# An unused tile that moves the squared activations by 640 bytes

## The chip, the cores and the metric

The kernel runs on one core of a Trainium2 chip. Its metric is device time, from the start of the program to its end, in microseconds (us). Three runs of the kernel before took 2282.85, 2284.05 and 2285.39 us; the median is 2284.05 us. Below, PE is the tensor engine (PEld its weight loads), DVE the vector engine, ACT the scalar engine, SP the engine whose queue issues the DMAs.

## The reference

Two layers of a decoder trunk on 256 tokens with 2048 features, in float32. Per layer:

```
mod = silu(c) @ w_ada + b_ada              # shift, scale, gate for the mixer and for the MLP
h   = rms_norm(x, g_pre_mix) * (1 + scale_a) + shift_a
y   = concat(mLSTM(h @ w_in), attention(h @ w_in)) @ w_out
x   = x + gate_a * rms_norm(y, g_post_mix)
h   = rms_norm(x, g_pre_mlp) * (1 + scale_m) + shift_m
y   = square(relu(h @ w_up)) @ w_down      # 2048 -> 8192 -> 2048
x   = x + gate_m * rms_norm(y, g_post_mlp)
```

The change is in the place of what `square(relu(h @ w_up))` is kept in. The two MLPs hold most of the arithmetic.

## The kernel before, in words

**Products in three parts.** Every large weight matrix streams from DRAM in loads of 1 MiB (128 partitions by 2048 columns, tile `raw`). A load is split in two slabs; of each slab, ACT makes a rounded copy `whi` (line 232) and DVE the rest `wlo = raw - whi` (line 236), both 128 by 1024 elements in the type float32r. Activations are kept in the same way, as a high and a low part. A product is the sum of three matmuls: high by high, low by high, high by low (lines 326 to 330, `products`; the matmul is line 329). Four tiles each of `whi` and `wlo` rotate, six of `raw`.

**Two forms of a unit.** A unit is one block of 512 weight columns, accumulated in two PSUM banks. In `body_xs` (line 332) the activations are stationary, 128 features by 128 tokens (512 bytes in each partition), and 512 columns of the slab move past them: this is the form of the output projection (`op`), of the down-projection (`dn`) and of a few units of the in-projection (`vm`, `om`). In `body_ws` (line 338) 128 columns of the slab are stationary and 256 tokens of the activations move: the form of the up-projection (`up`). Each matmul is preceded by the load of its own stationary operand.

**Order.** One list fixes the order of all loads, slabs and units. In the MLP the units alternate: for each of 8 stages `e`, one up unit (a block of 512 hidden features, 16 k-tiles), four down units (`dn`, 8 k-tiles each, one for each 512 output features), one more up unit. After an up unit, `evac_up` (line 1007) evacuates it: ACT takes the relu into the tile `r` and squares it into `sh`; DVE squares `r` in place and writes `sl = r - sh`. The down units read `sh` and `sl` as their stationary operands. In between, DVE also sums rows of `w_ada` (line 204), adds up the outputs of the down units (line 1064), and SP issues the loads.

**Where the tiles lie.** Pools are stacked in each partition's memory in the order in which they are opened. `raw`, `whi`, `wlo` and the normed activations `ht` (which also hold the concatenated heads, `cth` and `ctl`) lie one behind the other, each tile a whole number of 4096 bytes; all of them begin 1504 bytes into a page of 4096 bytes. Behind them come pools of other sizes, 32128 bytes together. Then the pools that live for one phase alone. For the MLP these are the two opened at lines 997 and 998:

```
sp = mlp.enter_context(tc.tile_pool(name="s" + L, bufs=3))   # sh, sl: six tiles of 4096 bytes
rp = mlp.enter_context(tc.tile_pool(name="r" + L, bufs=2))   # r: two tiles of 2048 bytes
```

Since 32128 is 640 less than eight pages, the six tiles of `sp` begin 864 bytes into a page, in both layers, and the two of `rp` at 864 and 2912. A stationary operand in `ht` begins 1504 bytes into a page plus a multiple of 512, one in `sp` 864 bytes plus a multiple of 512; the 512 columns of a slab begin at 1504 or 3552.

Of the kernel before, what the change touches and what calls it, by code (L numbers as in the profile page):

```python
# [7 lines left out]
F32 = mybir.dt.float32  # L8
# [6 lines left out]
PSUM = bass.MemoryType.PSUM  # L15
# [11 lines left out]

# column offsets in the packed small parameters
NL = 234
# [3 lines left out]

# shape-only constants: identity | banded distances | causal bias
K_ID, K_DIST, K_CAUS = 0, 128, 512
# [4 lines left out]
def hymba_kernel(ctx: ExitStack, tc: tile.TileContext, x_d, c_d, cols_d, cons_d, wada_d,  # L40
# [48 lines left out]

    # instructions behind which the splits and the sums of w_ada queue on their engine, lest they come  # L90
    # between the steps of a norm that the tensor engine waits for
    hold = {"hi": None, "lo": None, "ada": None}

    def rsqrt(ssq, n_over, n, name):
        """1 / sqrt(ssq / n_over + eps): an estimate from the exponent bits and three Newton steps."""
        v, y, t = [smp.tile([P, n], F32, tag=f"rs_{a}", name=f"{name}_{a}") for a in "vyt"]
        V.tensor_scalar(v, ssq, 1.0 / n_over, EPS, ALU.mult, ALU.add)
        V.tensor_scalar(y.bitcast(I32), v.bitcast(I32), -0.5, 1597463007.0, ALU.mult, ALU.add)
        V.tensor_scalar(v, v, -0.5, None, ALU.mult)
        for _ in range(3):  # L100
            if n == 1:
                V.tensor_scalar(t, y, y, v, ALU.mult, ALU.mult)
            else:
                V.tensor_tensor(t, y, y, ALU.mult)
                V.tensor_tensor(t, t, v, ALU.mult)
            last = V.scalar_tensor_tensor(y, t, 1.5, y, ALU.add, ALU.mult)
        hold["ada"] = last.ins
        return y

# [1 line left out]
    # ("w", blocks of (unit, first k-tile), source) of weights; ("a", layer, vector, pair of feature tiles) of w_ada  # L111
    SHA, SCA, GTA, SHM, SCM, GTM = range(6)
# [8 lines left out]
    def weave(ws, *segments):  # L121
        """ws, with the entries ads of each segment (ads, start, upto) spread evenly over that range of ws."""
        at = {}
        for ads, start, upto in segments:
            for k, a in enumerate(ads):
                at.setdefault(start + int(k * (upto - start) / len(ads)), []).append(a)
        for n, w in enumerate(ws):
            plan.append(w)
            plan.extend(at.pop(n, []))
        assert not at  # L130
# [32 lines left out]

    # each entry in two loads
    loads, subs, ada_fifo = [], [], []
# [13 lines left out]

# [1 line left out]
    LA, RING, AHEAD = 2, 4, 5  # L181
# [16 lines left out]
    def ada_op():  # L198
        """Sums over the input features for one tile of 128 output features."""
        k, l, v, j = ada_fifo.pop(0)  # L200
        load_to(k + AHEAD)
        w = raws[k]
        with behind("ada"):
            V.scalar_tensor_tensor(w, w, 1.0, cact, ALU.mult, ALU.mult, accum_out=modc[l][:, v, j:j + 1])  # L204
        n = modn[l, v] = modn.get((l, v), 0) + 1
        gate = v in (GTA, GTM)
        if n % (KT if gate else 2):
            return
        j0 = 0 if gate else n - 2
        m = modc[l][:, v, j0:n]  # L210
        V.tensor_tensor(m, m, lcol(l, O_BA + 16 * v + j0, n - j0), ALU.add)
        if v in (SCA, SCM):
            g = lcol(l, (O_GPM if v == SCA else O_GPL) + j0, n - j0)
            V.scalar_tensor_tensor(m, m, 1.0, g, ALU.add, ALU.mult)
        if gate:
            V.tensor_tensor(m, m, lcol(l, O_GQM if v == GTA else O_GQL, KT), ALU.mult)
# [31 lines left out]

# [1 line left out]
    class Task:  # L250
# [36 lines left out]
    class Unit:  # L287
        """Products with one block of 512 weight columns, accumulated in two PSUM banks."""

# [21 lines left out]
        def slabs_by_token(self, between):  # L311
            """Four slabs, all for the first token tile and then all for the second."""
            prefill(RING)
            four = [take() for _ in range(4)]
            for s in four:
                side()
                self.mm(s, toks=(0,))
            between()
            for s in four:
                self.mm(s, toks=(1,))  # L320
# [33 lines left out]

    # gate rows (times the post-norm gain) broadcast over the partitions
    gps = {}
# [14 lines left out]

# [1 line left out]
    class PreNorm:  # L373
        """Residual update (with yg), RMSNorm, modulation and transposition of x."""

# [33 lines left out]
        def group(self, g, tok):  # L409
            """Transposed activations of four k-tiles, in two parts."""  # L410
            tag, l = self.tag, self.l
# [17 lines left out]
        def turn_in(self, xnT, tok, g0=0):  # L429
            """Transposition of one token tile from k-tile 4 g0 on, before the modulation is known."""  # L430
            for g in range(g0, 4):
                ps = xalloc(f"pst{self.tag}_{g}_{tok}")
                for k in range(4):
                    T.transpose(ps[:, k * P:(k + 1) * P], self.xn[g, tok][:, k * P:(k + 1) * P], ident)
                o = xnT[g][:, :, TK[tok]]
                p4 = ps.rearrange("p (k t) -> p k t", k=4)
                if g % 2:
                    A.activation(o, p4, AF.Copy)
                else:
                    V.tensor_copy(o, p4)  # L440
                xdone()

        def modulate(self, e, xnT, hfp):
            """Two k-tiles of the activations."""
            tag, l, g = self.tag, self.l, e // 2
# [20 lines left out]
    def turn(last_mm, evac, nrm, make, staged=None):  # L466
        """Between two phases: the token tiles pass one after the other through the end of the last
        unit, the norms and the start of the first unit of the next phase. The first half of the
        k-tiles goes through all the units made, then the second half."""
        def mid():  # L470
# [35 lines left out]

# [1 line left out]
    crow = gpp.tile([P, D], F32, tag="gp", name="crow")[0:1, :]  # L508
# [15 lines left out]
    for l in range(DEPTH):  # L524
# [34 lines left out]

# [1 line left out]
        ha = {}  # L561
# [61 lines left out]
        def swa_out(g, po):  # L623
            """Normalisation of four heads and their sums of squares."""
            hs = slice(4 * g, 4 * g + 4)
# [59 lines left out]

# [1 line left out]
        def conv_silu(ps, u, out_scale):  # L687
# [24 lines left out]

# [1 line left out]
        wg = tp.tile([P, KT, 8], F32, tag="wg", bufs=1, name=f"wg{L}")  # L714
# [5 lines left out]
        def gates():  # L720
# [28 lines left out]
            xdone()  # L749
            # log sigmoid(f) = min(f, 0) - log1p(exp(-|f|)), log1p(t) = log(w) + (t - (w - 1)) / w with w = 1 + t  # L750
            V.scalar_tensor_tensor(t1, fg, -1.0, fg, ALU.mult, ALU.min)
# [14 lines left out]
            yield  # L766
            # u = i - b, g = running maximum of u (from the stabiliser before the chunk), m = b + g
            u_, m_, emm, g_, ub = both[0:4], lf, fg, t2, t1
# [8 lines left out]
            yield  # L777
            # columns: u (two chunks), u + B (first chunk), exp(-m) (two chunks)
            while live["x"] > 3:
# [8 lines left out]

# [1 line left out]
        va = {}  # L790
# [13 lines left out]
        def mlstm_weights(h):  # L804
            """exp(u_s - g_t) times q k, [source position, target position]."""
            pg = xalloc(f"pg{L}_{h}")
# [81 lines left out]

# [1 line left out]
        cg = {}  # L890
# [28 lines left out]

# [1 line left out]
        if l:  # L921
# [33 lines left out]

# [1 line left out]
        cT = lambda kt: (cg[kt // 4][0][:, kt % 4, :], cg[kt // 4][1][:, kt % 4, :])  # L957
# [35 lines left out]

# [1 line left out]
        hT2 = PreNorm("m" + L, l, SCM, SHM, yg, ssy)  # L995
        mlp = ExitStack()
        sp = mlp.enter_context(tc.tile_pool(name="s" + L, bufs=3))
        rp = mlp.enter_context(tc.tile_pool(name="r" + L, bufs=2))
# [22 lines left out]
        def evac_up_tokens(un, u):  # L1021
            """As evac_up, for products with tokens on the partitions."""
            ps = un.ps
# [180 lines left out]
```

## Time and profile before

| | |
|---|---|
| three runs, median | 2284.05 us (2282.85 to 2285.39) |
| profiled execution, span from first to last instruction (the page gives no other time for it) | 2283.6 us |
| mean granted clock of the tensor engine | 0.987 of full |
| PE, PEld, DVE, ACT busy | 96%, 85%, 74%, 48% of the span |
| chain that ended last, `up` and `dn` matmuls | 31.7% and 30.8% of the span |
| DMA | 590.08 MB, 258 GB/s mean |

The page gives the busy time of each engine. Matmuls are pipelined: the duration shown of one is its time from start to end, and the next has begun by then. How many fit in a stretch is read from the starts, or from the chain of waits, which lists stretches of one kind of instruction with their count. A "pitch" below is the time from one start to the next.

### The profile page before, as it was taken

The page shows a single profiled execution, that of the slowest core. Times are in us where ns is not written, and L with a number is a line of the kernel's source. Part 1 is how long each engine was busy: PE and PEld are TensorE (multiplying, and loading weights), DVE is VectorE, ACT ScalarE, POOL GpSimd, SP SyncE. Part 2 cuts the span into 40 slices and gives each one's busy share as a digit, 9 for nine tenths or more (in the row PEclk, how much of TensorE's full clock was granted, in tenths as well). Part 3 has the DMA queues.
Part 4 walks back from the last instruction along what each step waited for, and adds up shares of the span by engine and source line. Part 5 has one row for each costly group of instructions (what it writes and reads, how often), then busy time and mean ns, then how long its engine had stood idle before and what let it go on. Part 6 is the DMA issues. An engine that isn't in the chain of part 4 may idle for free.

```text
span 2283.6 us, 33092 instructions
## 1 busy us (share of the span) xinstructions
PE 2195.6 (96%) x13322; PEld 1935.3 (85%) x13322; DVE 1690.7 (74%) x2282; ACT 1090.9 (48%) x1533; POOL 1.4 (0%) x14
## 2 busy tenths in 40 slices
PE   6789999899999999999989999989999999999998
PEld 5679777698898998989869988878898998998986
DVE  7988899787878877877577797957556656555556
ACT  4346663645444444434464566556443444444433
POOL 0000000000000000000000000000000000000000
PEclk9999999999999999999999999999999999999999
DMA  9997679497888888888538766845656666555551
GB/s 370 385 360 273 221 300 365 171 356 307 315 299 336 308 309 312 316 305 300 185 128 336 294 223 215 294 165 197 234 213 230 229 223 248 203 185 186 184 187 70
DMA packets 82363, 590.08 MB, mean 258 GB/s; under 512 B 9185, under 2 KB 9633, under 8 KB 10785
## 3 DMA queue, kind: packets, MB, share of 16 engines
q1 hardware_dynamic: 82210, 587.98, 69.4%
q8 instruction: 104, 1.70, 0.3%
q14 instruction: 49, 0.40, 0.0%
HBM read 585.81 MB, written 2.13 MB: 257 GB/s over the span
## 4 chain that ended last, share of the span: by engine, by line
PE 77%; DVE 4%; ACT 1%; issue 1%; DVEq 0%; ACTq 0%
PE up L329 32%; PE dn L329 31%; PE op L329 4%; PE qa L329 2%; PE vm L329 2%; PE om L329 1%; PE km L329 1%; PE qm L329 1%; PE kva L329 1%; DVE x L388 1%; DVE wlo L236 1%; PE pss L592 0%; PE pss L591 0%; ACT jkm L84 0%; PE psgate L730 0%
## 5 line engine op out<-in xcount | busy, mean ns | idle before, releaser
L236 DVE TENSOR_TENSOR wlo<-raw,whi 128x1024 fp32r<-128x1024 f32 x720 | 876.6, 1222 | 472.2 <-ACT whi L232 470.9
L232 ACT ACTIVATE whi<-raw 128x1024 fp32r<-128x1024 f32 x720 | 758.5, 1058 | 915.3 <-PE dn L329 376.0
L329 PE MATMUL up<-hthm,whi 128*128 128x256 f32 x1920 | 543.7, 283 | 0.0
L329 PE MATMUL up<-hthm,wlo 128*128 128x256 f32 x1920 | 543.3, 283 | 0.0
L329 PE MATMUL up<-htlm,whi 128*128 128x256 f32 x1920 | 543.2, 283 | 0.0
L204 DVE SCALAR_TENSOR_TENSOR raw<-raw,cact 128x2048 f32<-128x2048 f32 x192 | 437.3, 2285 | 4.1 <-DMA raw<-in_wada_dram 4.0
L329 PE MATMUL dn<-whi,sh 128*128 128x512 f32 x1024 | 404.1, 395 | 0.0
L329 PE MATMUL dn<-wlo,sh 128*128 128x512 f32 x1024 | 404.0, 395 | 0.0
L329 PE MATMUL dn<-whi,sl 128*128 128x512 f32 x1024 | 404.0, 395 | 0.0
L329 PEld LDWEIGHTS up<-htlm,whi 128*128 128x128 f32 x1920 | 368.4, 192 | 0.9
L329 PEld LDWEIGHTS up<-hthm,whi 128*128 128x128 f32 x1920 | 368.4, 192 | 0.9
L329 PEld LDWEIGHTS up<-hthm,wlo 128*128 128x128 f32 x1920 | 368.4, 192 | 0.0
L329 PEld LDWEIGHTS dn<-wlo,sh 128*128 128x128 f32 x1024 | 192.9, 188 | 45.0
L329 PEld LDWEIGHTS dn<-whi,sh 128*128 128x128 f32 x1024 | 193.0, 188 | 44.7 <-ACT sh L1034 0.4
L329 PEld LDWEIGHTS dn<-whi,sl 128*128 128x128 f32 x1024 | 192.9, 188 | 44.4 <-DVE sl L1035 0.2
L329 PE MATMUL op<-wlo,cth 128*128 128x512 f32 x256 | 99.6, 395 | 2.8 <-DVE wlo L236 2.8
L329 PE MATMUL op<-whi,cth 128*128 128x512 f32 x256 | 99.2, 396 | 2.6 <-ACT whi L232 2.6
L329 PE MATMUL op<-whi,ctl 128*128 128x512 f32 x256 | 100.2, 393 | 0.0
L329 PE MATMUL vm<-whi,htha 128*128 128x512 f32 x128 | 57.0, 447 | 28.7 <-ACT whi L232 18.7
L1064 DVE TENSOR_TENSOR ys<-ys,dn 128x512 f32<-128x512 f32 x112 | 75.4, 685 | 5.2 <-PE dn L329 4.6
L329 PE MATMUL qa<-htha,whi 128*128 128x256 f32 x256 | 73.2, 286 | 0.0
L329 PE MATMUL qa<-htla,whi 128*128 128x256 f32 x256 | 72.4, 283 | 0.0
(275 smaller groups left out, 2545.1 us busy)
## 6 DMA issues: line engine op xcount, KB each, us to landing
raw<-in_wada_dram SPq DMA_DIRECT2D x192, 1024.0 KB, 6.4
raw<-in_wdn_dram SPq DMA_DIRECT2D x128, 1024.0 KB, 5.0
raw<-in_wup_dram SPq DMA_DIRECT2D x120, 1024.0 KB, 4.9
raw<-in_win_dram SPq DMA_DIRECT2D x56, 1024.0 KB, 5.0
raw<-in_wout_dram SPq DMA_DIRECT2D x32, 1024.0 KB, 6.8
raw<-in_wst_dram SPq DMA_DIRECT2D x16, 1024.0 KB, 6.6
raw<-in_wsu_dram SPq DMA_DIRECT2D x8, 1024.0 KB, 6.2
gp<-gdr SPq DMA_DIRECT2D x4, 1024.0 KB, 4.7
```

What stands on the lines that cost most here:

```text
L204: V.scalar_tensor_tensor(w, w, 1.0, cact, ALU.mult, ALU.mult, accum_out=modc[l][:, v, j:j + 1])
L232: A.activation(hi, raw, AF.Copy)
L236: V.tensor_tensor(lo, raw, hi.bitcast(F32), ALU.subtract)
L329: T.matmul(o, a, w, start=not self.started[b], stop=last and i == 2, skip_group_check=True)
L388: V.scalar_tensor_tensor(xc, self.yg[c][tok], r, xc, ALU.mult, ALU.add)
L1064: V.tensor_tensor(yt, yt, ps[tok], ALU.add)
```

## The change

Ahead of the pool of the squared activations, a pool is opened that holds one tile of 160 float32 (640 bytes) in each partition. No instruction reads or writes it. It is open as long as the MLP of its layer. The pools `sp` and `rp` lie 640 bytes further up: the six tiles of `sp` begin 1504 bytes into a page, the two of `rp` at 1504 and 3552. No other tile moves. The rest of the diff takes comments away.

```
         hT2 = PreNorm("m" + L, l, SCM, SHM, yg, ssy)
         mlp = ExitStack()
+
+        mlp.enter_context(tc.tile_pool(name="page" + L, bufs=1)).tile([P, 160], F32, name=f"page{L}")
         sp = mlp.enter_context(tc.tile_pool(name="s" + L, bufs=3))
         rp = mlp.enter_context(tc.tile_pool(name="r" + L, bufs=2))
```

On all five engines the same instructions stand in the same order as before, with the same waits; only the addresses of `sh`, `sl`, `r` and of the tiles that borrow their places in layer 0 (`xnT`, `hfs`) differ.

## Rows read from the trace of the kernel before

**Rows 1.** The page: busy time and share of each engine.
```profile
PE 2195.6 (96%) x13322; PEld 1935.3 (85%) x13322; DVE 1690.7 (74%) x2282; ACT 1090.9 (48%) x1533; POOL 1.4 (0%) x14
```

**Rows 2.** The chain that ended last, stretches: start us, length us, what, count.
```profile
533.12 0.44 PE up L1032 x4
533.55 44.87 PE dn L329 x192
601.46 44.62 PE dn L329 x192
...
1122.63 39.05 PE dn L329 x168
...
1465.47 58.96 PE op L329 x259
...
1660.62 46.07 PE up L329 x384
...
2160.21 44.62 PE dn L329 x192
2204.83 23.03 PE up L329 x192
2227.86 39.05 PE dn L329 x168
```

**Rows 3.** Who waited for whom: engine, line, releaser; us in total, times, longest.
```profile
ACT whi L232 <- PE dn L329: 376.0, 224, 1.7
ACT whi L232 <- PE up L329: 355.3, 200, 1.9
```

**Rows 4.** One down stage, PE: durations min/median/max in ns, first and last start.
```profile
L329 PE MATMUL dn<-whi,sh x64: 390/393/404, 1706.5 to 1750.4; 128*128 128x512 f32 x64
L329 PE MATMUL dn<-whi,sl x64: 390/393/404, 1706.8 to 1750.7; 128*128 128x512 f32 x64
L329 PE MATMUL dn<-wlo,sh x64: 390/393/404, 1707.0 to 1750.9; 128*128 128x512 f32 x64
```

**Rows 5.** The same view of the output projection of layer 1.
```profile
L329 PE MATMUL op<-whi,ctl x84: 389/389/393, 1467.1 to 1523.8; 128*128 128x512 f32 x84
L329 PE MATMUL op<-wlo,cth x84: 389/389/389, 1467.4 to 1523.3; 128*128 128x512 f32 x84
L329 PE MATMUL op<-whi,cth x83: 389/389/389, 1467.6 to 1523.6; 128*128 128x512 f32 x83
```

**Rows 6.** Timeline of weight loads in a down stage: start us, length us, what.
```profile
1625.13 0.19 PEld L329 LDWEIGHTS dn<-wlo,sh 128*128 128x128 f32 x1
1625.37 0.19 PEld L329 LDWEIGHTS dn<-whi,sh 128*128 128x128 f32 x1
1625.60 0.19 PEld L329 LDWEIGHTS dn<-whi,sl 128*128 128x128 f32 x1
...
1626.76 0.19 PEld L329 LDWEIGHTS dn<-whi,sh 128*128 128x128 f32 x1
1627.00 0.19 PEld L329 LDWEIGHTS dn<-whi,sl 128*128 128x128 f32 x1
```

**Rows 7.** Stretches: start:end, length, busy us (count) by engine, clock, DMA share, GB/s.
```profile
783.00:827.50 44.50, 44.50 (x193) 36.09 (x192) 37.85 (x43) 18.56 (x20) 0.00 (x0) 1.00 0.87 323
1467.00:1524.00 57.00, 57.00 (x253) 47.19 (x252) 34.66 (x35) 24.70 (x33) 0.00 (x0) 1.00 0.70 250
1706.70:1751.30 44.60, 44.60 (x194) 36.15 (x194) 30.87 (x31) 18.66 (x20) 0.00 (x0) 1.00 0.65 235
```

**Rows 8.** DVE lines: shapes, count | busy us, mean ns | idle before.
```profile
L1016 DVE TENSOR_TENSOR sl<-r,sh 128x512 fp32r<-128x512 f32 x60 | 41.3, 689 | 1.2
L427 DVE TENSOR_TENSOR htlm<-hfm,hthm 128x512 fp32r<-128x512 f32 x12 | 8.2, 687 | 5.0 <-ACT hthm L426 5.0
```

More of the change, by code (lines that the diff above doesn't have):

```diff
@@ L996, in hymba_kernel @@
         mlp = ExitStack()
+        mlp.enter_context(tc.tile_pool(name="page" + L, bufs=1)).tile([P, 160], F32, name=f"page{L}")
         sp = mlp.enter_context(tc.tile_pool(name="s" + L, bufs=3))
```

## The prediction

> **What bounds the kernel now.** The page comes first: PE is busy for 96% of the span, the next engine, DVE, for 74% [rows 1]. A busy share alone doesn't show a bound, so the chain of waits comes next. In the MLPs it is PE without a break: stretches of `dn` and `up` follow each other to the hundredth of a microsecond, as at the end, where 2160.21 + 44.62 is 2204.83, the start of the next, and 2204.83 + 23.03 is 2227.86 to within rounding [rows 2]. The list of waits says the same from the other side: ACT, the first of the two engines that make the slabs, waits 376.0 us for `dn` matmuls and 355.3 us for `up` matmuls to set a slab's place free [rows 3]. It is ahead of PE, not behind. So a nanosecond that is taken from a matmul of these stretches is taken from the end, up to the point where the slabs are late.
>
> **What the change does, part by part.** It removes nothing, adds no instruction and no wait, and moves none past another, on the queues of SP and POOL neither. All it can change is how long an instruction takes that touches a moved tile. These are of four kinds: the 3072 matmuls of the down units with the loads of their stationary operand, the writers of `sh`, `sl` and `r` on ACT and DVE, the transposes of `r` by PE for one up unit of each layer, and the few modulation steps that borrow these tiles.
>
> *The down matmuls.* The chain has 14 stretches of 192 of them, one of 44.87 us (the first, with its start) and thirteen of 44.62, and two of 168 with 39.05 us each [rows 2]. That is 13 x 44.62 + 44.87 + 2 x 39.05 = 703.0 us for 14 x 192 + 2 x 168 = 3024 matmuls, 232.5 ns each. The missing 48 of 3072 are those of the second token tile in the last unit of each layer, which run beside the evacuation of the first and are not on the chain. One stage read by its starts gives the same: from 1706.5 to 1750.9 lie 191 steps, 232.5 ns each [rows 4].
>
> The question is what this pitch is made of, and the trace has the control experiment in it. The output projection is the same form of unit: the same line, the same three products in the same order, 128 by 128 stationary, 512 columns moving, two PSUM banks in turn, slabs from the same tiles. From 1467.1 to 1523.8 its 251 matmuls make 250 steps, 226.8 ns each [rows 5]. In both stretches the granted clock is 1.00, the level of 2.4 GHz [rows 7], and in both PE has no idle time. Two things differ. First, in `op` the stationary operand lies in `ht` tiles, which have the slabs' place in a page (1504), and in `dn` in `sp` tiles, 640 bytes off it. Second, `sp` lies higher up in the memory than `ht`, by 32128 bytes and more.
>
> The shape of the slower pitch speaks for a conflict in time and not for a longer read as such. In `op` the durations are 389 ns at minimum and at median, and hardly vary. In `dn` they run from 390 to 404 [rows 4, 5], and the starts of the weight loads come at steps of 0.23 us with one of 0.24 us about every seventh: from 1625.13 to 1625.37, and again from 1626.76 to 1627.00 [rows 6]. It is a beat: the weight load slides against the moving operand until something makes it wait. That is what I expect of two reads that get in each other's way at some relation of their addresses, and in `op` don't. Nor does it look like the height in memory: the six tiles of `sp` span 24 KiB, `sh` and `sl` change places between the layers, and the stretches of both layers are 44.62 us, to the digit [rows 2]. After the change the stationary operands have, within a page, exactly the places that those of `op` have. I take the pitch of `op` for them.
>
> At 226.8 ns, 3024 matmuls take 685.8 us, 17.2 us less than 703.0. Some of it is lost at the entry of a stretch: the whole `op` stretch, entry with its waits for slabs included, is 58.96 us for 259, 227.6 ns each [rows 2]; at that mean the gain is only 14.7 us. An entry costs at each of 16 stretches, not at each matmul, so I stay near the steady figure and take 0.4 us off: 16.8 us. The bounds of this term, if it is the place in the page, are 14.7 and 17.2.
>
> *The writers.* `r`, `sh` and `sl` move together, so their relation to one another stays. `sl` is made at 689 ns with all its operands at the old place, and the same shape in the norm takes 687 ns with its operands at others [rows 8]: over 60 of them 0.1 us, off the chain as long as PE is ahead. I count nothing. Were DVE's or ACT's writers 5% slower (35 ns on 689), a hidden 2 us in all would be lost to idle time that these engines have. The transposes of `r` are eight per layer at 0.44 us for four [rows 2]: nothing.
>
> *What hides what next.* If the slabs of a down stage are used up sooner, they have to be made sooner. A down stage of layer 0 takes 43.5 us instead of 44.5; DVE's work in it, 37.85 us with the sums of `w_ada`, is then 87% of it instead of 85%, and DMA would move 330 GB/s instead of 323 [rows 7]. In layer 1 DVE has 30.87 us of work in a stage. Both still fit.
>
> Sum: 2283.6 - 16.8 = 2266.8 us of span. The median of the runs is 0.45 us above the profiled span; so 2267.2 us for the median.
>
> The Trainium skill, in "TensorE: Matmul & The Clock Gate", Part 2 (what happens when you issue a matmul), says that PE has two independent read ports into SBUF, and that loading the next stationary operand takes no read bandwidth from the running matmul; "SBUF — State Buffer", section "Who interferes with whom", lists PE among the engines that wait for no one. By that rule no relation of addresses matters, the change does nothing, and the time stays at 2284.1. No run shown here disproves it, but it leaves the difference of 232.5 and 226.8 ns between two stretches of one form without a cause [rows 4, 5].
>
> **The rivals.**
>
> *It is not the place in the page: no change.* The pitch of `dn` stays at 232.5 ns and the time at 2284.1. For it: only one pair of stretches carries the contrast, and `sp` differs from `ht` in its height too. Against it: both layers, with `sh` and `sl` exchanged, are alike, and six other tiles' worth of height made no difference within `sp`.
>
> *Only part arrives.* The slabs become the bound in layer 0, where DVE is at 85% of a down stage and the DMA engines at 0.87 [rows 7]. Then layer 0 keeps its 44.6 us stages and only layer 1 gains: half of 16.8, a time of 2275.6. Against it: ACT's waits for PE are spread over 424 places [rows 3], so the supply has a reserve almost everywhere.
>
> *Slower: equal places collide.* If reads conflict where two addresses agree within a page, as in a memory of interleaved banks, the change brings the two operands onto each other. Its place is the weight load of each down matmul. Its price: now one step in about seven is 0.24 us; with the conflict at every matmul all of them are, 3024 x (240 - 232.5) ns = 22.7 us, a time of 2306.7. It decides from a pitch of 233 ns on. Against it: `op` and `up` have their operands at equal places already, `op` at 226.8 ns.
>
> **How the numbers follow.** The forecast, the pitch of `op` in all down stages: 0.74, with a range of its own from 2264 (the steady gain, and the 1.3 us by which runs differ from their median) to 2270 (the gain of 14.7). Part of it: 0.07. No change: 0.12. Slower: 0.07. A change under 0.2% (4.6 us) can't be told from none in this kernel. The first two are both faster by more: 0.81; same 0.12; slower 0.07. The range takes in the forecast and the partial case, 2263 to 2278, and leaves out the other two.
>
> **What would show it.** Right: in the chain, `dn` stretches of 43.5 to 43.6 us for 192 and 38.1 for 168; durations of 389 ns at minimum and median; no steps of 0.24 us; `up` stretches still 46.07 us; ACT still waiting for `dn` matmuls. Wrong: `dn` stretches of 44.6 us (the place isn't the cause), or of 46 (it collides); or stretches of 43.5 with new gaps in front of `up` in layer 0, where PE would wait for `whi` or `wlo` (the supply).

## The result and the profile after

The changed kernel takes 2267.06 us (median of four runs, 2266.08 to 2270.54), the kernel before 2283.77 us in the runs that belong to it (four, 2282.85 to 2285.39). The ratio is 0.9927, with a 95% interval of [0.9913, 0.9941]: 16.7 us or 0.7% faster.

The chain that ended last, in the changed kernel (start us, length us, what, count), at the places of [rows 2]:

```profile
535.42 43.85 PE dn L329 x192
...
602.31 43.55 PE dn L329 x192
...
1117.08 38.12 PE dn L329 x168
...
1459.05 58.95 PE op L329 x259
...
1653.14 46.07 PE up L329 x384
...
2147.40 43.55 PE dn L329 x192
2190.95 23.03 PE up L329 x192
2213.98 38.12 PE dn L329 x168
```

Every down stretch is shorter, by 1.07 us for 192 matmuls (1.02 in the first stretch) and 0.93 us for 168; `op` and `up` have kept their lengths. Thirteen stretches of 43.55, one of 43.85 and two of 38.12 make 686.24 us, where 703.03 us were: 16.79 us less. PE works through these stretches without a gap, as before.

One down stage of the changed kernel by its durations (ns, minimum/median/maximum, first and last start in us), against [rows 4]:

```profile
L329 PE MATMUL dn<-whi,sh x64: 389/389/396, 1699.0 to 1741.9; 128*128 128x512 f32 x64
L329 PE MATMUL dn<-whi,sl x64: 389/389/398, 1699.3 to 1742.1; 128*128 128x512 f32 x64
L329 PE MATMUL dn<-wlo,sh x64: 389/389/389, 1699.5 to 1742.4; 128*128 128x512 f32 x64
```

The 390, 393 and 404 ns have become 389 at minimum and median, the figure of `op` [rows 5]; from first to last start 191 steps take 43.4 us, 227 ns each. And its weight loads on the timeline, where [rows 6] had the step of 0.24 us:

```profile
1625.10 0.19 PEld L329 LDWEIGHTS dn<-whi,sl 128*128 128x128 f32 x1
1625.32 0.19 PEld L329 LDWEIGHTS dn<-wlo,sh 128*128 128x128 f32 x1
1625.55 0.19 PEld L329 LDWEIGHTS dn<-whi,sh 128*128 128x128 f32 x1
1625.78 0.19 PEld L329 LDWEIGHTS dn<-whi,sl 128*128 128x128 f32 x1
1626.00 0.19 PEld L329 LDWEIGHTS dn<-wlo,sh 128*128 128x128 f32 x1
```

All steps are 0.22 or 0.23 us. Four steps would not show a beat that comes about every seventh, but read in nanoseconds the trace has the 184 steps between weight loads from 1700 to 1742 us all at 226 or 227. The beat is gone.

The spans of the two profiled executions differ by 14.8 us (2283.6 and 2268.8), not by 16.8. The first down stretch begins at 533.55 before and at 535.42 after: 1.87 us are lost ahead of it, and they are lost already where the last stretch of `op` in layer 0 begins (403.22 and 405.09), ahead of the MLP and its moved tiles. In the runs below the start of the first down stretch lies between 531.76 and 536.02 us and follows no edit. So whole times of single runs are compared only to some 4 us, and the stretches of the chain carry the verdicts.

### The profile page after: what moved, and what is told of

It reads as the page before. It is cut to its first block, busy times and chain, and to the rows that moved or that the text cites. A ratio compares the mean times of both kernels' runs of the same rounds, so it can differ in the third digit from the quotient of the medians.

```text
span 2268.8 us, 33092 instructions
## 1 busy us (share of the span) xinstructions
PE 2180.5 (96%) x13322; PEld 1935.3 (85%) x13322; DVE 1688.3 (74%) x2282; ACT 1091.1 (48%) x1533; POOL 1.4 (0%) x14
## 4 chain that ended last, share of the span: by engine, by line
PE 86%; DVE 10%; ACT 2%; issue 1%; DMA 0%; SPq 0%; DVEq 0%; ACTq 0%
PE up L329 32%; PE dn L329 30%; PE op L329 6%; DVE raw L204 4%; PE vm L329 3%; PE om L329 3%; PE qa L329 3%; DVE wlo L236 2%; PE km L329 2%; PE qm L329 2%; PE kva L329 1%; DVE x L388 1%; PE pss L592 1%; PE pss L591 1%; PE psgate L730 0%
## 5 line engine op out<-in xcount | busy, mean ns | idle before, releaser
L329 PE MATMUL dn<-whi,sh 128*128 128x512 f32 x1024 | 398.7, 389 | 0.0
L329 PE MATMUL dn<-whi,sl 128*128 128x512 f32 x1024 | 398.6, 389 | 0.0
L329 PE MATMUL dn<-wlo,sh 128*128 128x512 f32 x1024 | 398.4, 389 | 0.0
```

Of the source, the lines that this page charges most:

```text
L329: T.matmul(o, a, w, start=not self.started[b], stop=last and i == 2, skip_group_check=True)
```

## The experiments

The stretches compared below are those of 192 down matmuls, where nothing else is named; "distance" is the place of `sh` and `sl` less the place of the slabs, -640 bytes in the kernel before and 0 in the changed one, up to whole pages.

**Which of the two moved pools counts.** The change moves `s` and `r`. Two kernels move one of them. The first:

```
         sp = mlp.enter_context(tc.tile_pool(name="s" + L, bufs=3))
+        mlp.enter_context(tc.tile_pool(name="page" + L, bufs=1)).tile([P, 160], F32, name=f"page{L}")
         rp = mlp.enter_context(tc.tile_pool(name="r" + L, bufs=2))
```

> The unused tile lies behind the pool of sh and sl, so that only r moves by 640 bytes; sh and sl stay at 864 in a page. Theory (the place of the stationary operand against the slab sets the pitch of the down matmuls): dn stretches stay at 44.62 us for 192, time as before, 2284 us. Rival (the gain comes with r, from its writers on ACT and DVE or its transposes): dn stretches of 43.55 us, 2267 us.

The second has the tile of the change ahead of `sp`, and this behind it:

```
         sp = mlp.enter_context(tc.tile_pool(name="s" + L, bufs=3))
+        mlp.enter_context(tc.tile_pool(name="back" + L, bufs=1)).tile([P, 864], F32, name=f"back{L}")
         rp = mlp.enter_context(tc.tile_pool(name="r" + L, bufs=2))
```

> The 640 bytes ahead of sh and sl as in the change, and a second unused tile of 3456 bytes behind them that puts r back to 864 and 2912 in a page. Theory (place of the stationary operand): dn stretches of 43.55 us, 2267 us, all of the change's gain. Rival (r): 44.62 us, 2284 us.

With `r` alone: 2284.95 us beside 2284.97 for the kernel before, ratio 1.0002 [0.9992, 1.0011]. With `s` alone: 2268.18 us, ratio 0.9929 [0.9914, 0.9944]. In the chain of the first and then of the second, the same stage of layer 0 and one of layer 1:

```profile
781.14 44.62 PE dn L329 x192
...
1614.21 44.62 PE dn L329 x192
```

```profile
779.04 43.55 PE dn L329 x192
...
1607.28 43.55 PE dn L329 x192
```

The gain is that of `sh` and `sl`, all of it; the place of `r` is worth nothing that these runs show.

**Page, 512 or 256 bytes.** The two layers open their pools apart, so one kernel tries two distances:

```
-.tile([P, 160], F32, name=f"page{L}")
+.tile([P, (32, 96)[l]], F32, name=f"page{L}")
```

> The unused tile has 128 bytes in layer 0 and 384 bytes in layer 1: sh and sl lie 512 bytes before the slabs' place in a page in layer 0, 256 bytes before it in layer 1. If the whole 4096-byte page counted, both layers keep 44.62 us for 192 dn matmuls (2284 us). If the distance counts modulo 512 bytes alone (the k-tile and token offsets within the tiles are multiples of 512 and made no difference): layer 0 has 43.55 us, layer 1 has not (2275 us). If it counts modulo 256: both have 43.55 us (2267 us).

Measured 2267.54 us (one run), with both layers fast:

```profile
778.58 43.55 PE dn L329 x192
...
1606.60 43.55 PE dn L329 x192
```

The page of 4096 bytes does not count, and not 512 either: a distance of 512 or 256 bytes is as good as none. It also settles the height in memory. In layer 0 the tiles lie 128 bytes above those of the kernel before and have the whole gain.

**Own place or distance.** Everything from the slabs up is moved by 128 bytes, with no tile in the MLP:

```
+    pool("low").tile([P, 32], F32, name="low")
     rawp = pool("raw", bufs=6)
```

> An unused tile of 128 bytes ahead of the pool of raw, none in the MLP: slabs, ht, sh, sl, r and the rest all lie 128 bytes further up. Slabs and ht begin at 1632 in a page, sh and sl at 992; their distance is 640 as before. Theory (the distance of the two operands counts): dn stays at 44.62 us for 192, op at 226.8 ns, up at 46.07 us for 384, time 2284 us. Rival (the stationary operand's own place modulo 512 counts, 480 fast and 352 slow): sh and sl now are at 480 modulo 512, so dn takes 43.55 us; ht is at 96, and op and up may become slower.

Measured 2285.13 us (before, same chip: 2284.97). The lines of this kernel are one further down:

```profile
782.59 44.62 PE dn L330 x192
827.20 46.07 PE up L330 x384
...
1465.17 58.99 PE op L330 x259
```

Here `sh` and `sl` have modulo 512 the place that they have in the changed kernel, and are slow; `ht` has another than before, and is fast. What counts is the distance of the two operands, not the place of one.

**The reverse, and the form of `up`.** The tile of 128 bytes between slabs and `ht`, none in the MLP:

```
+    pool("low").tile([P, 32], F32, name="low")
     htp = pool("ht", bufs=4)
```

> No unused tile in the MLP, but one of 128 bytes between the slabs and the pool ht: ht is then 128 bytes off the slabs' place, as sh and sl were before, and sh and sl are 512 bytes off it. Theory (distance modulo 256 of the two operands of any such matmul): dn at 43.55 us for 192; the form of op goes to 232.5 ns, its stretch of 259 from 58.95 to 60.4 us, and so the few vm, om and first up units; for the form of up, slab stationary and ht moving, this is its first trial at another distance: if its 120.0 ns suffer in proportion (2.5%), a stretch of 384 has 47.2 us and the kernel 2267 + 18 + 8 = 2293 us; if that form has no conflict, 46.07 us and 2275 us. Rival (something in sp alone): dn as before at 44.62 us, op unchanged.

Measured 2272.69 us (before, same chip: 2282.31):

```profile
781.54 43.56 PE dn L330 x192
825.11 46.08 PE up L330 x384
...
1459.57 60.63 PE op L330 x259
...
1586.19 25.63 PE up L330 x216
```

Now `dn` is fast and `op` is slow: 60.63 us for 259, expected 60.4. The loss is not one of the down units; it goes to whichever unit of the form `body_xs` has its operands 128 bytes apart. It is not the same to the digit: the steady pitch of `op` is 233.3 ns here, with steps of 229 to 238, against 232.4 in the down units of the kernel before. Why is not known.

The form of `up`, with 256 columns moving, keeps 46.08 us for 384, 120.0 ns each, so 2293 us fell and 2275 was the nearer expectation. But this form is not untouched. In the changed kernel the starts in its stretch at 1653.14 are 120 ns apart, with one of 119; here, in the stretch at 1655.39, they are 117 to 123 apart, with the same mean. And its stretches of 216 got faster, 118.7 ns a matmul. That of the changed kernel:

```profile
1583.67 25.92 PE up L329 x216
```

The stretch of 216 of `qa` in layer 1, of the same form, went from 25.92 to 25.63 us as well. Why the stretches of 384 don't gain, no run shows.

**Finer distances.** Three kernels with other sizes of the unused tile, two distances each.

> The unused tile has 704 bytes in layer 0 and 576 in layer 1: sh and sl lie 64 bytes behind the slabs' place (modulo 256) in layer 0, 64 bytes before it in layer 1. Theory X, only a distance of whole 256 bytes is free: 44.62 us for 192 dn matmuls in both layers, 2284 us. Theory Y, the loss grows with the distance up to 128: about 44.1 us in both, 2276 us. Theory Z, the distance counts in blocks of 128 bytes, so that less than that is free: 43.55 us in both, 2267 us. If the order of the two reads in time counts, the two layers differ.

> The same with 672 and 608 bytes: 32 bytes behind the slabs' place in layer 0, 32 before it in layer 1. X: 44.62 us in both layers, 2284 us. Y: about 43.8 us, 2271 us. Z: 43.55 us, 2267 us.

> The same with 736 and 544 bytes: 96 bytes behind the slabs' place in layer 0, 96 before it in layer 1. X: 44.62 us in both layers, 2284 us. Y: about 44.35 us, 2280 us. Z: 43.55 us, 2267 us.

In the chains, a stage of layer 0 and one of layer 1 each, with 704 and 576 bytes:

```profile
783.87 44.80 PE dn L329 x192
...
1707.80 43.95 PE dn L329 x192
```

with 672 and 608 bytes:

```profile
604.09 44.79 PE dn L329 x192
...
1664.57 46.07 PE up L329 x384
1710.64 44.80 PE dn L329 x192
```

and with 736 and 544 bytes:

```profile
783.95 44.98 PE dn L329 x192
...
1709.88 44.80 PE dn L329 x192
```

Whole times, one run each: 2281.96, 2290.57 and 2289.78 us, the kernel before 2282.31 on that chip. The second's first down stretch began 536.02 us after the start, the latest of all runs and 2.47 later than in the kernel before, which is a part of its 2290.57. In the third the 16 down stretches of the chain are 4.24 us longer in sum than those of the kernel before.

Theory X is nearest: already 32 bytes of distance, on either side, cost as much as 128, and a little more: 44.79 and 44.80 us where X said 44.62. The loss does not grow with the distance (Y fell), and no block of 128 bytes is free (Z fell). X missed one of six: 576 bytes, 64 before the slabs' place, have 43.95 us. A last kernel asks whether that is a matter of that layer or place:

```
-.tile([P, 160], F32, name=f"page{L}")
+.tile([P, (80, 112)[l]], F32, name=f"page{L}")
```

> The unused tile has 320 bytes in layer 0 and 448 bytes in layer 1: distances of -320 and -192 bytes to the slabs' place, which are -64 and +64 modulo 256, realised by 256 bytes less and in exchanged layers. If the distance counts modulo 256 in its fine steps too: 43.95 us for 192 dn matmuls in layer 0 and 44.80 us in layer 1. If the 43.95 us at 576 bytes had to do with layer 1 or with that very place: other values, such as 44.8 us in layer 0.

```profile
779.21 43.95 PE dn L329 x192
...
1699.96 44.80 PE dn L329 x192
```

Measured 2279.84 us (before, same chip: 2286.08), and the two values as expected, in exchanged layers. The table of the distance modulo 256, with all eight values that tiles laid at multiples of 32 bytes can have:

| distance modulo 256 | 0 | 32 | 64 | 96 | 128 | 160 | 192 | 224 |
|---|---|---|---|---|---|---|---|---|
| us for 192 | 43.55 | 44.79 | 44.80 | 44.98 | 44.62 | 44.80 | 43.95 | 44.80 |

At 32, 96, 160 and 224 each value comes from one layer of one run. For the down matmuls no distance beats 0, so no version better than the changed kernel follows from the table.

**Whose reads.** In layer 1 the down units take no slabs of their own, with the tiles where they were before:

```
+        if unit[0] == "dn" and unit[1] == 1:
+            splits[s] = (unit, kt, *last_split)
+            st["split"] += 1
+            return
```

> Tiles as in the kernel before (no unused tile, sh and sl at 864 in a page). In layer 1 the down units are not given slabs of their own: ACT and DVE split nothing for them, and their matmuls read the slab that was split last; what they compute is left out so far. ACT and DVE then hardly touch the memory in these stretches (the additions of the down outputs and what up units ask for remain), the matmuls are the same. Theory (the two reads of PE itself, weight load and moving operand, get in each other's way): 44.62 us for 192 in layer 1 as in layer 0. Rival (the weight load or the moving operand waits for ACT's and DVE's accesses to slabs that lie at another place in a page): layer 1 falls towards 43.55 us.

Measured 2287.41 us (before, same chip: 2286.08). The chain of this kernel, then its stretches (start:end, length, busy us and count of PE, PEld, DVE, ACT, POOL, clock, DMA share, GB/s) in layer 0 and in layer 1:

```profile
1618.05 44.62 PE dn L334 x192
1662.66 46.07 PE up L334 x384
1708.73 44.62 PE dn L334 x192
```

```profile
783.00:827.00 44.00, 44.00 (x198) 36.04 (x198) 37.15 (x42) 18.54 (x21) 0.00 (x0) 1.00 0.87 327
1707.00:1750.00 43.00, 43.00 (x194) 35.18 (x193) 14.55 (x17) 5.42 (x7) 0.00 (x0) 1.00 0.40 165
```

Layer 1 has less work of DVE and the DMAs from the start, so the stretch to compare with is that of layer 1 in the kernel before [rows 7]. Against it ACT's work has gone from 18.66 to 5.42 us, DVE's from 30.87 to 14.55 and the DMA engines' share from 0.65 to 0.40, while the stretch is 44.62 us in both, with steps of 228 to 241 ns as before. A loss that the other engines or the DMAs made would have shrunk with their work; they don't make the slow pitch.

## Why the prediction was right

**What bounds it.** The chain stayed on PE, and the gain of a stretch reached the end. ACT still waits for PE to set the slabs' places free, 17.4 us less than in [rows 3] behind `dn`:

```profile
ACT whi L232 <- PE dn L329: 358.6, 223, 1.7
ACT whi L232 <- PE up L329: 358.6, 202, 1.9
```

**The down matmuls.** Forecast 16.8 us, between 14.7 and 17.2; measured in the chain 16.79. The step that carried it was to read `op` as the control for `dn`: the same line of code, tile shapes and clock, another place of one operand, 226.8 against 232.5 ns. The 0.4 us for the entries of the stretches was of the right size: 686.24 us for 3024 matmuls are 226.9 ns each.

**The beat.** The uneven starts [rows 6] were taken for two reads that get in each other's way, and not for one longer read. The runs that move both operands, one of them, or the other bear out that their distance decides. With much less work of the other engines the slow pitch stayed. That leaves the two reads of PE itself, the load of a stationary operand and the moving operand; that these two delay each other is concluded from this and not seen. How the memory is built that 256 bytes come out is not shown by any run. The picture of one step in seven that waits was too simple. In nanoseconds, from 1707 to 1750 us of the kernel before, 26 of 184 steps between the starts of matmuls are 240 or 241, but the others are 228 to 233 and not the 226 or 227 of `op`. The long steps hold about a third of the loss; the rest lies on the steps between them, each longer than any regular step of `op`.

**The place in the page.** The forecast was right, but its condition was stricter than needed. It expected the gain because the places within the page become those of `op`; the runs show that 256 bytes are enough to look at.

**The writers, and what hides what.** `sl` takes 690 ns where it took 689 [rows 8], and the kernel that moves `r` alone has the time of the kernel before. DVE and the DMA engines carry the shorter stages, as worked out: a stage of layer 0 of the changed kernel, and one of layer 1, against [rows 7]:

```profile
781.70:825.10 43.40, 43.40 (x193) 35.92 (x192) 37.51 (x42) 18.52 (x20) 0.00 (x0) 1.00 0.88 328
1699.30:1742.70 43.40, 43.40 (x193) 35.95 (x192) 30.63 (x31) 18.51 (x20) 0.00 (x0) 1.00 0.67 240
```

DVE is busy for 86% of the stage in layer 0 (87% forecast), DMA moves 328 GB/s (330 forecast).

**The sum.** The forecast of 2267.2 us is the median of before, 2284.05, less 16.8: the 0.45 us between the profiled span and the median is taken off and put back. It is not what lies around a span: the runs of the changed kernel have 1.7 us around theirs (2270.54 us for the profiled one of 2268.8), so the profiled execution of before was probably the slowest of its runs. Against that execution the forecast would have been 2268.5, and 2270.54 came, 1.87 us of it lost ahead of the first down stretch. That the median, 2267.06, lies within 0.2 us of the forecast is in part luck: the four runs of the changed kernel spread over 4.5 us. The 16.79 us of the chain are the firmer agreement.

**The rivals.** *No change* falls with the result. *Only part arrives* falls: both layers have 43.55 us. *Equal places collide* falls the other way round: for the down matmuls equal places are, modulo 256 bytes, the only ones without loss, and 32 bytes apart is as slow as 128. Its price, 240 ns for every step, was too high as well; the slowest stretch of all eight distances, 44.98 us, is 0.36 us above that of the kernel before.

The rule of the Trainium skill that was weighed, "TensorE: Matmul & The Clock Gate", Part 2, that loading the next stationary operand takes no read bandwidth from the running matmul, was read to mean that no relation of addresses matters. That does not hold here for 128 by 128 operands with 512 columns moving in this four-byte type: 5.6 ns of each matmul (1.07 us over 192) hang on the distance of their addresses. Nor does it hold to the letter for the form with 256 columns: its stretches of 384 take 46.07 or 46.08 us at both distances, but its stretches of 216 take 25.92 us at 0 bytes and 25.63 at 128. Whether it is read bandwidth that is lost, no run shows.

## What to carry to other kernels

Where two stretches of one form of matmul have different pitches, compare everything that differs between them, the places of their tiles included, before the slower one is taken for the hardware's pace. For this form, with 512 columns moving, lay the stationary and the moving operand a multiple of 256 bytes apart; an unused tile of the right size does it. As the distance decides, moving the pool of the slabs should do as well as moving that of the activations; no run moved the slabs alone. For the form with 256 columns the same distance was not the fastest in every stretch, so it has to be measured there. A pad in one pool moves all pools above it, so a change of some tile's size elsewhere can take such a gain away, or bring it.

## What the runs showed of the hardware

The pitch of float32r matmuls with a stationary operand of 128 by 128 and 512 moving columns, at a granted clock of 1.00, is 226.8 ns where the operands are a multiple of 256 bytes apart, 228.9 at 192 modulo 256 and 232.4 to 234.3 at the other six distances (stretches of 192: 43.55, 43.95 and 44.62 to 44.98 us). With 256 moving columns it was 120.0 ns at 0 bytes; at 128 bytes it was 120.0 in stretches of 384 and 118.7 in stretches of 216 (25.63 us against 25.92). The table is not symmetric: 64 bytes before the slab's place cost 0.40 us on a stretch, 64 behind it 1.25 us. I had expected neither the 256 bytes nor that.
